# Operands of a blocked triangular inverse: two wide tiles filled by two engines, and the fourth pair's substitution on VectorE

## The chip, the cores and the metric

The kernel runs on one core of one Trainium2 chip. The metric is the device time of one execution in microseconds, the median of three runs. TensorE (PE) does matmuls, VectorE (DVE), ScalarE (ACT) and GpSimd (POOL) the elementwise work, SyncE (SP) issues the transfers.

## The reference

One layer of a hybrid backbone over 640 tokens (128 context, 512 latent), width 1024: one input projection, a bidirectional gated DeltaNet with 8 heads, a convolution branch, gates, an output projection and a SwiGLU block. What matters here is the DeltaNet: in each chunk a unit lower triangular system is solved.

```python
decay = jnp.exp(jnp.where(incl, gc[..., :, None] - gc[..., None, :], -jnp.inf))
a_mat = jnp.where(strict, jnp.einsum('bhnik,bhnjk->bhnij', kb, k) * decay, 0.0) \
    + jnp.eye(CHUNK, dtype=jnp.float32)
sol = lax.linalg.triangular_solve(a_mat, rhs, left_side=True, lower=True, unit_diagonal=True)
```

## The kernel before, in words

Heads are worked in four pairs. A pair has 20 matrices of 128x128 (2 directions d, 2 heads, 5 chunks) in the tile `Bt`, each to be inverted. `pair_prep` builds `Bt` (GpSimd sets its diagonal, line 590), takes the 32x32 diagonal blocks of all 20 into `Cc` (lines 598 and 599), transposes them into `M` (601) and inverts them by forward substitution: 30 steps of two elementwise instructions each (lines 610 and 612) on `X`, each step on the result of the one ahead. The table `SUBST_V` says which engine does them: VectorE for the first three pairs, GpSimd for the fourth. Two transposes (616, 617) leave the block inverses as `T1` and `T2`.

`pair_inverse` sets the 32x32 inverses into block diagonal 128x128 operands, `XA` and `XB`, in float16, one tile of four matrices for each of five lanes: a memset of `XA` on GpSimd (625) and the copies of line 631 on ScalarE. `XB` is zeroed once, at line 447. Each lane (`invert`) then takes six steps: GpSimd takes the part of `Bt` outside the diagonal blocks into `ct` (654); two products with `XA`, put into `a` and `atr` by ScalarE (665, 666); a product with `XB`, added to `XB` by VectorE (668), and a square put back into the lane's own `XA` (669); a third product (671); a transpose (675, 677) and the residual, by VectorE (678); the last product into `Bt` (680). All these matmuls but the last two steps' are of line 660. `pair_scan` uses the result (716 to 766), and `pair_out` follows.

In between runs the dense work, above all the projections: `load_w` fetches a weight tile `wr`, ScalarE rounds it to `wh` and VectorE or GpSimd takes the remainder `wl` (109, 110), and 48 matmuls of line 147 follow for each of some 50 column blocks. Their results leave through ScalarE and VectorE (873 and 875 for the gate `tz`, 882 for `tgt`); the convolution's 31 taps (847, 850 and 854) run on VectorE.

Generators (`preps`, `inverses`, `scans`, `mains` and others) are run turn about by the weights `W_...` that they yield; what a pair's chain issues has a higher priority than the dense work. A scheduler with a timeline of its own then fixes each engine's order of instructions when the kernel is built. On the chip every engine takes its list in that order and waits where an operand isn't ready.

## Time and profile before

| | before |
|---|---|
| median of 3 runs | 1381.05 us (1378.54 to 1384.46) |
| profiled execution, its own time | 1383.22 us |
| its span | 1381.2 us |
| PE, DVE, ACT, POOL busy | 94%, 61%, 39%, 22% |
| PE busy between 200 and 300 us | 80.97 us |
| PE busy between 900 us and the end | 470.99 of 481.20 us |

Busy shares are means over the span. The work that this case is about lies between 140 and 820 us; from 900 us on stand the feed-forward blocks. Since PE takes its list in order, what counts is where it stands idle, for whom it waits there, and at what clock it runs afterwards (the profile's column PEclk is the clock that was granted, 1.00 being full speed).

### The profile page before, as it was taken

To read this page: it belongs to the slowest core of one execution; us is meant where nothing else is said; L and a number is where in the kernel's file an instruction comes from. 1 tells how busy PE (TensorE), PEld (TensorE's weight loads), DVE (VectorE), ACT (ScalarE), POOL (GpSimd) and SP (SyncE) were. 2 spreads that over 40 slices of the span, in tenths; PEclk is the share of its full clock that TensorE was granted. 3 is DMA by queue.
4 is the path that set the end of the run, shared out by engine and by line. 5 is a ranking of instruction groups with operands and counts; after the bars stand their busy time and mean duration, and the time that the engine had idled before them with its cause. 6 is when DMAs were issued, how large, how long until landed. Compare 5 with 4: busy or idle time off the path is not lost.

```text
span 1381.2 us, 23408 instructions
## 1 busy us (share of the span) xinstructions
PE 1291.9 (94%) x9180; PEld 1213.3 (88%) x9180; DVE 839.1 (61%) x1603; ACT 542.0 (39%) x1240; POOL 306.8 (22%) x354
## 2 busy tenths in 40 slices
PE   4998996978999998988999989999999999999997
PEld 4998895977998998888989988889998999989996
DVE  5788985978667899596577774731223321233236
ACT  3337647263454555526454133332221222212223
POOL 2103310200010310291010025433310333003314
PEclk8999998999999999998999999999999999999999
DMA  9523442343343543323346884122222222222222
GB/s 289 140 64 113 125 149 80 112 136 100 113 119 99 160 118 94 103 66 94 118 150 212 250 284 148 46 74 77 77 77 76 77 77 77 76 76 69 71 77 91
DMA packets 180334, 157.31 MB, mean 114 GB/s; under 512 B 9072, under 2 KB 151809, under 8 KB 180225
## 3 DMA queue, kind: packets, MB, share of 16 engines
q1 hardware_dynamic: 180225, 155.83, 36.5%
q8 instruction: 72, 1.18, 0.4%
q14 instruction: 37, 0.30, 0.1%
HBM read 131.80 MB, written 24.00 MB: 113 GB/s over the span
## 4 chain that ended last, share of the span: by engine, by line
PE 68%; DVE 13%; ACT 6%; DMA 5%; issue 4%; POOL 1%; SPq 1%; POOLq 0%; DVEq 0%; ACTq 0%
PE mm L147 46%; PE sm L1115 9%; PE mm L1115 4%; DMA wr<-in_w_in 3%; ACT XA L631 2%; ACT XB L631 2%; PE sm L660 2%; DVE wl L110 1%; DVE uacc L847 1%; DVE acc L484 1%; PE sm L736 1%; ACT wh L109 1%; PE sm L495 1%; PE mm L469 1%; DMA og<-ogd 1%
## 5 line engine op out<-in xcount | busy, mean ns | idle before, releaser
L109 ACT ACTIVATE wh<-wr 128x1024 fp32r<-128x1024 f32 (+1 forms) x154 | 152.6, 992 | 497.5 <-PE mm L147 209.3
L147 PE MATMUL mm<-hh,wh 128*128 128x256 f32 (+1 forms) x896 | 219.7, 320 | 11.6 <-ACT wh L109 7.8
L147 PE MATMUL mm<-hl,wh 128*128 128x256 f32 (+1 forms) x896 | 218.0, 317 | 0.0
L147 PE MATMUL mm<-hh,wl 128*128 128x256 f32 (+1 forms) x896 | 216.4, 317 | 0.0
L110 POOL TENSOR_TENSOR wl<-wr,wh 128x1024 fp32r<-128x1024 f32 (+1 forms) x59 | 133.2, 2260 | 345.9 <-ACT wh L109 337.5
L110 DVE TENSOR_TENSOR wl<-wr,wh 128x1024 fp32r<-128x1024 f32 (+1 forms) x95 | 110.0, 1158 | 126.0 <-ACT wh L109 114.9
L147 PEld LDWEIGHTS mm<-hh,wh 128*128 128x128 f32 x896 | 163.5, 192 | 17.7 <-ACT wh L109 8.3
L147 PE MATMUL mm<-h2h,wh 128*128 128x256 f32 (+1 forms) x704 | 165.0, 312 | 1.5 <-ACT h2h L109 1.5
L147 PEld LDWEIGHTS mm<-hl,wh 128*128 128x128 f32 x896 | 166.3, 192 | 0.0
L147 PE MATMUL mm<-h2l,wh 128*128 128x256 f32 (+1 forms) x704 | 164.9, 312 | 0.9 <-POOL h2l L110 0.9
L147 PEld LDWEIGHTS mm<-hh,wl 128*128 128x128 f32 x896 | 164.6, 191 | 0.5 <-DVE wl L110 0.2
L147 PE MATMUL mm<-h2h,wl 128*128 128x256 f32 (+1 forms) x704 | 164.3, 311 | 0.3 <-DVE wl L110 0.3
L1253 DVE TENSOR_TENSOR ft<-ft,mm 128x384 f32<-128x384 f32 (+1 forms) x44 | 19.7, 484 | 198.8 <-PE mm L147 198.6
L147 PEld LDWEIGHTS mm<-h2l,wh 128*128 128x128 f32 x704 | 130.5, 191 | 1.1 <-POOL h2l L110 1.1
L147 PEld LDWEIGHTS mm<-h2h,wh 128*128 128x128 f32 x704 | 129.2, 190 | 1.9 <-ACT h2h L109 1.7
L147 PEld LDWEIGHTS mm<-h2h,wl 128*128 128x128 f32 x704 | 130.0, 190 | 0.6 <-DVE wl L110 0.6
L484 DVE SCALAR_TENSOR_TENSOR acc<-ci,colA,acc 128x642 f32<-128x642 f32 x96 | 85.9, 895 | 7.8 <-ACT acc L482 7.2
L1115 PE MATMUL sm<-wh,fl 128*128 128x512 f32 x152 | 60.0, 395 | 0.0
L1115 PE MATMUL sm<-wh,fh 128*128 128x512 f32 x152 | 59.9, 394 | 0.0
L1115 PE MATMUL sm<-wl,fh 128*128 128x512 f32 x152 | 59.7, 392 | 0.0
L110 DVE TENSOR_TENSOR fl<-ft,fh 128x640 fp32r<-128x640 f32 x22 | 47.7, 2167 | 15.5 <-ACT fh L109 15.5
L847 DVE SCALAR_TENSOR_TENSOR uacc<-u,colB,uacc 128x113 f32<-128x113 f32 (+14 forms) x120 | 47.8, 399 | 0.9
(341 smaller groups left out, 2431.7 us busy)
## 6 DMA issues: line engine op xcount, KB each, us to landing
wr<-in_w_in SPq DMA_DIRECT2D x56, 512.0 KB
wr<-in_w_gu SPq DMA_DIRECT2D x44, 512.0 KB
wr<-in_w_ada SPq DMA_DIRECT2D x32, 512.0 KB
wr<-in_w_down SPq DMA_DIRECT2D x22, 512.0 KB
wada<-in_w_ada SPq DMA_DIRECT2D x8, 1024.0 KB
atd<-et SPq DMA_DIRECT2D x40, 128.0 KB
aux<-atd SPq DMA_DIRECT2D x40, 128.0 KB
tgd<-tgt SPq DMA_DIRECT2D x16, 320.0 KB
```

The lines of the kernel that those rows point to most:

```text
L109: S_.activation(hi, x, AF.Identity)
L110: return (lo_eng or V).tensor_tensor(out=lo, in0=x, in1=hi.bitcast(F32), op=ALU.subtract)
L147: PE.matmul(out, a[:, kt, :], x, start=(kt == 0 and j == 0), stop=(kt == nk - 1 and j == 2))
L469: PE.matmul(pa[32 * g:32 * g + 32, :], sc[:, kt, o:o + 32], w[:, c:c + P], start=(bb == 0), stop=(bb == 1), tile_position=(0, 32 * g))
L484: V.scalar_tensor_tensor(out=acc[:, :n], in0=ci[:, k:k + n], scalar=vA[:, k, ct:ct + 1], in1=acc[:, :n], op0=ALU.mult, op1=ALU.add)
L495: PE.transpose(pt[:, c, :], src(c0 + c), ident)
L631: S_.activation(dst[r, o:o + cnt, 32 * b:32 * b + 32], src[r, :, n0:n0 + cnt].rearrange("p o n -> p n o"), AF.Identity)
L660: PE.matmul(pt[:, j, :], lhs[j], rhs[:, j, :], start=True, stop=True)
L736: PE.matmul(pv[:, d, j, :], Y1[:, d, j, ck[d], :], rhs, start=True, stop=True)
L847: V.scalar_tensor_tensor(out=acc[:, a0:128 - a1], in0=u[:, a0 + dl:128 - a1 + dl], scalar=tap(k, t4), in1=acc[:, a0:128 - a1], op0=ALU.mul ...
L1115: PE.matmul(acc[i], a[kt // 4][:, kt % 4, c], b[:, k2, :], start=(kt == 0 and j == 0), stop=(kt == nk - 1 and j == 2))
L1253: V.tensor_tensor(out=d, in0=d, in1=s, op=ALU.mult)
```

## The change

`XA` and `XB` become one tile each for all five lanes, indexed by direction and matrix, and each 32-row block is filled by one copy of 10 matrices: 8 copies for `XA` on ScalarE and 8 for `XB` on GpSimd, in place of 48 smaller ones on ScalarE. A lane takes its four matrices as a slice. The memset of `XA` becomes one instruction, that of `XB` too. The table `SUBST_V` goes, and all four substitutions are VectorE's.

```diff
-SUBST_V = (1, 1, 1, 0)
...
-    XA = [const(f"XA{i}", [P, 4, P], F16, s1p) for i in range(5)]
-    XB = [const(f"XB{i}", [P, 4, P], F16, s1p) for i in range(5)]
-    for t in XB:
-        G.memset(t, 0.0)
+    XA, XB = (const(nm, [P, 2, 10, P], F16, s1p) for nm in ("XA", "XB"))
+    G.memset(XB.rearrange("p d n i -> p (d n i)"), 0.0)
...
-            (V if SUBST_V[p] else G).tensor_tensor(out=t, in0=bc(M[:, j + 1:, j:j + 1], [P, n, j]), in1=bc(X[:, j:j + 1, 0:j], [P, n, j]),
+            V.tensor_tensor(out=t, in0=bc(M[:, j + 1:, j:j + 1], [P, n, j]), in1=bc(X[:, j:j + 1, 0:j], [P, n, j]),
                             op=ALU.mult)
-            (V if SUBST_V[p] else G).tensor_tensor(out=X[:, j + 1:, 0:j], in0=X[:, j + 1:, 0:j], in1=t, op=ALU.add)
+            V.tensor_tensor(out=X[:, j + 1:, 0:j], in0=X[:, j + 1:, 0:j], in1=t, op=ALU.add)
...
-        groups = [((0, 4, k % 2, 4 * (k // 2)),) for k in range(4)] + [((0, 2, 0, 8), (2, 2, 1, 8))]
-        for k, parts in enumerate(groups):
-            G.memset(XA[k], 0.0)
-            for o, cnt, d, n0 in parts:
-                n0 += 10 * d
-                for b in range(4):
-                    r = slice(32 * b, 32 * b + 32)
-                    for dst, src in ((XA[k], T1 if d == 0 else T2), (XB[k], T2 if d == 0 else T1)):
-                        S_.activation(dst[r, o:o + cnt, 32 * b:32 * b + 32],
-                                      src[r, :, n0:n0 + cnt].rearrange("p o n -> p n o"), AF.Identity)
-            yield W_BUILD
+        G.memset(XA.rearrange("p d n i -> p (d n i)"), 0.0)
+        for d in range(2):
+            for b in range(4):
+                r = slice(32 * b, 32 * b + 32)
+                S_.activation(XA[r, d, :, 32 * b:32 * b + 32],
+                              (T1, T2)[d][r, :, 10 * d:10 * d + 10].rearrange("p o n -> p n o"), AF.Identity)
+                G.tensor_copy(XB[r, d, :, 32 * b:32 * b + 32],
+                              (T2, T1)[d][r, :, 10 * d:10 * d + 10].rearrange("p o n -> p n o"))
+            yield 2.5 * W_BUILD
...
-            xa, xb = XA[k], XB[k]
...
+                xa, xb = XA[:, d, n0:n0 + 4, :], XB[:, d, n0:n0 + 4, :]
...
+                xa, xb = XA[:, :, 8:10, :], XB[:, :, 8:10, :]
```

The lists of the engines change with it. In the rows below a line of the changed kernel is 1 to 4 lower than the same line before (109 is 108, 738 is 734, 873 is 869, 665 is 661, 678 is 674, 847 is 843, 654 is 653, 612 is 609, and 631 is 624 on ScalarE and 626 on GpSimd).

ScalarE at the first pair's build. Before, the last of 48 copies and what stood behind them (`Cc` belongs to the second pair's preparation):

```order
L631 ACTIVATE XA_684<-T_1592 32x2x32
L631 ACTIVATE XB_689<-T_1591 32x2x32
L665 ACTIVATE L_672<-sm 128x512
L666 ACTIVATE L_673<-sm 128x512
L598 ACTIVATE Cc<-Bt 32x320 x4
L873 ACTIVATE tz<-mm 128x256
L873 ACTIVATE tz<-mm 128x384
```

Now, from the weights ahead of the copies to the first products:

```order
L108 ACTIVATE wh<-wr_59 128x1024
L624 ACTIVATE XA<-T_1579 32x10x32 x4
L869 ACTIVATE tz<-mm 128x256
L624 ACTIVATE XA<-T_1580 32x10x32 x4
L595 ACTIVATE Cc<-Bt 32x320 x4
L869 ACTIVATE tz<-mm 128x384
L108 ACTIVATE wh<-wr_55 128x1024
L661 ACTIVATE L_672<-sm 128x512
```

Eight copies stand where 48 stood, and the gate's first half is taken out between them.

ScalarE at the second pair's build, before (the first pair's scan has begun; `vn` is its):

```order
L631 ACTIVATE XA_684<-T_2552 32x2x32
L631 ACTIVATE XB_689<-T_2551 32x2x32
L109 ACTIVATE wh<-wr_59 128x1024
L738 ACTIVATE vn<-sm 128x512
L873 ACTIVATE tz<-mm 128x256
L873 ACTIVATE tz<-mm 128x384
```

and now:

```order
L108 ACTIVATE wh<-wr_59 128x1024
L734 ACTIVATE vn<-sm 128x512
L624 ACTIVATE XA<-T_2503 32x10x32 x4
L624 ACTIVATE XA<-T_2504 32x10x32 x4
L869 ACTIVATE tz<-mm 128x256
L869 ACTIVATE tz<-mm 128x384
```

The weights `wh` and the scan's `vn` have moved from behind the copies to ahead of them.

VectorE at the third pair's residuals (678, now 674), beside which the fourth pair's substitution runs. Before, the third and the fourth residual, among the convolution's taps (847):

```order
L678 TENSOR_TENSOR L_678<-sm,ident 128x512
L847 SCALAR_TENSOR_TENSOR uacc<-u,colB,uacc 128x116
L847 SCALAR_TENSOR_TENSOR uacc<-u,colB,uacc 128x115
L847 SCALAR_TENSOR_TENSOR uacc<-u,colB,uacc 128x114
L847 SCALAR_TENSOR_TENSOR uacc<-u,colB,uacc 128x113
L110 TENSOR_TENSOR wl_60<-wr_59,wh 128x1024
L678 TENSOR_TENSOR aux<-sm,ident 128x512
```

and now the same two:

```order
L674 TENSOR_TENSOR L_678<-sm,ident 128x512
L850 SCALAR_TENSOR_TENSOR uacc<-u,colB,uacc 128x448
L607 TENSOR_TENSOR stmp<-M,X 128x238
L843 SCALAR_TENSOR_TENSOR uacc<-u,colB,uacc 128x121
L850 SCALAR_TENSOR_TENSOR uacc<-u,colB,uacc 128x384
L609 TENSOR_TENSOR X<-X,stmp 128x17x14
L843 SCALAR_TENSOR_TENSOR uacc<-u,colB,uacc 128x122
L850 SCALAR_TENSOR_TENSOR uacc<-u,colB,uacc 128x320
L607 TENSOR_TENSOR stmp<-M,X 128x240
L843 SCALAR_TENSOR_TENSOR uacc<-u,colB,uacc 128x123
L674 TENSOR_TENSOR aux<-sm,ident 128x512
```

The substitution's steps (607, 609) now alternate with pairs of taps. Between the start of the fourth pair's substitution and the fourth residual stood 44 taps; now 21 taps and 29 steps of the substitution stand there.

## The prediction, as put on record before the changed kernel ran

> **What bounds the kernel now.** I read the page's busy shares first, then PE's own waits, then ScalarE's groups and timeline around the longest of them, and last a table of windows for the granted clock.

> ```profile
> PE 1291.9 (94%) x9180; PEld 1213.3 (88%) x9180; DVE 839.1 (61%) x1603; ACT 542.0 (39%) x1240; POOL 306.8 (22%) x354
> ```

> PE is the bound and has 1381.2 - 1291.9 = 89 us idle in its span. The change touches no matmul, so it can only give or take such idle time, and what the clock loses after it. The list of PE's waits (in all, times, longest) shows whom it waits for:

> ```profile
> PE mm L147 <- ACT wh L109: 8.9, 3, 7.1
> PE sm L566 <- ACT K L540: 6.5, 1, 6.5
> PE sm L660 <- ACT XA L631: 5.2, 2, 3.8
> ...
> PE mm L147 <- DVE tz L875: 3.8, 1, 3.8
> PE sm L660 <- DVE aux L678: 3.5, 1, 3.5
> PE sm L736 <- ACT Sn L749: 3.4, 1, 3.4
> ...
> PE sm L660 <- ACT L L665: 2.9, 1, 2.9
> PE sm L660 <- DVE L L678: 2.8, 2, 2.0
> ```

> Only one of these names the copies of line 631, but the others stand behind them. ScalarE's timeline at the second pair (start, us, engine, line), and PE's at the same place, show how:

> ```profile
> 275.78 0.44 ACT L631 ACTIVATE XA<-T 32x128 f16<-32x128 f32 x1 [5.21 <-DVE T L616]
> ...
> 291.31 0.29 ACT L631 ACTIVATE XB<-T 32x64 f16<-32x64 f32 x1
> 291.62 1.06 ACT L109 ACTIVATE wh<-wr 128x1024 fp32r<-128x1024 f32 x1
> ```
> ```profile
> 292.73 0.90 PE L147 MATMUL mm<-hh,wh 128*128 128x256 f32 x2 [7.08 <-ACT wh L109]
> ```

> For 15.84 us (275.78 to 291.62) ScalarE does nothing but copies, and the weights `wh` that PE needs stand behind the 48th. The third pair's 6.5 us (`K`, line 540) and the fourth's 3.4 us (`Sn`, line 749, which stands among the last copies) are of the same kind; the first pair's 5.2, 2.9 and 3.8 us are waits for the copies, for the first evacuation behind them, and for a gate that ScalarE took late. The windows behind the five places give the price that isn't in the list, the clock (columns: window, length, busy of each engine, PEclk, DMA):

> ```profile
> 221.00:237.00 16.00, 9.27 (x60) 8.15 (x60) 8.99 (x19) 13.23 (x31) 1.26 (x1) 0.57 0.23 75
> 290.00:298.00 8.00, 5.27 (x22) 5.04 (x23) 4.81 (x11) 4.07 (x12) 0.00 (x0) 0.57 0.70 233
> 552.00:560.00 8.00, 4.90 (x27) 4.28 (x26) 1.64 (x2) 7.91 (x25) 0.00 (x0) 0.57 0.22 84
> 620.00:628.00 8.00, 4.22 (x25) 4.09 (x25) 6.49 (x11) 0.00 (x0) 6.02 (x15) 0.57 0.21 82
> 648.00:656.00 8.00, 6.52 (x28) 6.53 (x29) 5.10 (x14) 6.49 (x21) 0.00 (x0) 0.57 0.36 117
> ```

> In each PE is granted 0.57 of its clock, so of its busy time 43% is lost: 4.0, 2.3, 2.1, 1.8 and 2.8 us.

> **The copies.** ScalarE's groups, shapes apart (count | busy, mean ns):

> ```profile
> L631 ACT ACTIVATE XA<-T 32x128 f16<-32x128 f32 x64 | 26.1, 425 | 9.7 <-DVE T L616 9.1
> L631 ACT ACTIVATE XB<-T 32x128 f16<-32x128 f32 x64 | 25.1, 413 | 0.1
> L631 ACT ACTIVATE XA<-T 32x64 f16<-32x64 f32 x32 | 9.7, 302 | 0.2
> L598 ACT ACTIVATE Cc<-Bt 32x320 f32<-32x320 f32 x16 | 7.5, 466 | 1.1 <-POOL Bt L590 1.0
> ```

> A copy of 32x320 with the strided read of line 631 isn't in the trace. From below it costs the 0.47 us of the same size in runs of 32 (line 598); from above 2.5 copies of 128, 1.06 us. The slope from 64 to 128 elements, (425 - 302)/64 = 1.9 ns, carried on from 425 gives 0.79 us, and I take that, for it is the same read. Eight are 6.3 us where 15.8 us stood: ScalarE is free 9.5 us sooner at each of four pairs.

> What becomes of the waits:
> - First pair: 5.2 + 2.9 + 3.8 = 11.9 us idle. `XA` of a direction is whole after four copies, 3.2 us; few matmuls stand between the lanes' first products, so up to 2 x 3.2 us of waiting can stay and none need; I keep 5. Gain 6.9, and the clock's 4.0, since none of the five windows lies behind waits as short as these would be.
> - Second pair: `wh` and `vn` now stand ahead of the copies. 7.1 + 2.3 = 9.4. Late next is the gate behind eight copies, but PE has a block of 48 matmuls in hand.
> - Third pair: `K` stands behind eight copies and one half gate instead of 48 copies. 6.5 + 2.1 = 8.6.
> - Fourth pair: `Sn` is now ahead of the copies. 3.4 + 2.8 = 6.2.

> [...]

> **The substitution.** On GpSimd it held the shared work of both engines back. Windows of the taps' two lines alone (DVE busy and count), while GpSimd ran the substitution and after it, and windows of the substitution's own tile `stmp` (DVE, then POOL):

> ```profile
> 580.00:627.00 47.00, 17.29 (x30) 0.94 0.24 74
> 638.00:662.00 24.00, 4.43 (x13) 0.86 0.40 119
> ```
> ```profile
> 580.00:627.00 47.00, 12.64 (x14) 0.94 0.24 74
> 638.00:662.00 24.00, 6.12 (x12) 0.86 0.40 119
> ```
> ```profile
> 468.00:535.00 67.00, 19.92 (x60) 0.00 (x0) 1.00 0.44 127
> 579.00:628.00 49.00, 0.00 (x0) 35.00 (x60) 0.93 0.23 71
> ```
> ```profile
> 577.00:633.00 56.00, 48.40 (x381) 46.43 (x380) 48.48 (x73) 15.99 (x28) 45.50 (x72) 0.94 0.22 66
> ```

> Taps of line 847 take 17.29/30 = 0.58 us beside GpSimd and 4.43/13 = 0.34 alone; those of 854 0.90 and 0.51. So the 44 taps get 7.1 + 5.5 = 12.6 us shorter, and the 60 steps cost VectorE 19.9 us (the third pair's row; 35.0 on GpSimd). Net +7.3 us on a VectorE that is busy 48.5 of 56 us: it fills up and just fits, so the transposes 616 and 617 come about when they did. What moves is the residual. Ahead of its fourth stand 11 and 10 taps and 29 steps, 11 x 0.34 + 10 x 0.51 + 29 x 0.33 = 18.4 us, where 29.9 us of taps stood: 11 us sooner, and PE waited 3.5 + 2.0 us there. Gain 5.5 + 1.8 = 7.3 us. Were the taps not to get shorter, the fourth pair would be 12.6 us later.

> **GpSimd's copies.** A GpSimd copy isn't in the trace. Rows that bound it:

> ```profile
> L654 POOL TENSOR_TENSOR L<-Bt,off 128x512 f16<-128x512 f32 x12 | 16.1, 1357 | 0.2 <-DVE L L671 0.2
> L604 POOL TENSOR_SCALAR_AFFINE_SELECT X<-M 128x1024 f32<-128x1024 f32 x4 | 6.9, 1734 | 32.3 <-DVE M L601 32.3
> L612 POOL TENSOR_TENSOR X<-X,stmp 128x234 f32<-128x234 f32 x2 | 2.5, 1250 | 0.1
> ```

> Per element 1.7, 2.7 and 5.3 ns, so 320 elements take 0.54 to 1.7 us; I take line 654's 0.85, which also writes float16. Eight are 6.8 us (4.3 to 13.7). `XB` is first read late:

> ```profile
> 208.04 1.21 DVE L617 STREAM_TRANSPOSE T<-X 128x1024 f32<-128x1024 f32 x1
> ```
> ```profile
> 236.34 0.40 PE L660 MATMUL sm<-XB,L 128*128 128x128 f16 x4
> ```

> 27.1 us after the transpose's end, 17.6 when ScalarE's 9.5 are off. The copies are hidden behind that, and the cover is gone at 2.2 us each. [...] While they run, VectorE's taps are slower by 0.58/0.34: up to 0.7 x 6.8 = 4.7 us a pair, 19 in all, none if PE waits for no tap; PE rarely does, so I take 4. The memsets are the same bytes.

> **What a faster PE runs into.** ScalarE already waits for weights:

> ```profile
> ACT wh L109 <- DMA wr<-in_w_in: 40.9, 19, 11.9
> ```

> A PE that is 40 us ahead asks for these sooner. Between nothing and all of 40.9 I take 5, because PE itself waits for `wh` three times only.

> **The sum.** 10.9 + 9.4 + 8.6 + 6.2 + 7.3 = 42.4, less 4 and 5, is 33 us. The profiled execution took 1383.2 us (span 1381.2, 2.0 around it), 2.2 above the median; 1383.2 - 33 = 1350.

> **The rivals.**
> - *The weights take over.* PE catches up with the loads, and what the first two places give is waited for again at the next `wh`. Against it: PE has only 8.9 us of waits for `wh`, 7.1 of them behind the copies. About half is left, 16 us: 1367.
> - *VectorE becomes the bound at the fourth pair.* Taps stay long or the steps wait for each other, the transposes come 12.6 us late, and PE idles for the fourth scan; the residual's 7.3 are not gained either. 33 - 20 = 13 us: 1370. For it: VectorE at 48.5 of 56 us; against: the taps' two rows.
> - *No change.* PE reaches the same later waits, on the scans, at the same time. Against it: between 650 and 800 us PE stands idle little. 1381.
> - *Slower: GpSimd's copies are late.* PE waits for `XB` in its list, 8p - 17.6 us at each of four pairs. At p = 2.2 us it begins, and 33 + 7 us are eaten at p = 3.5 us; at 4 us it is 58 - 33 = 25 us slower, 1406. Against it: the slowest row gives 1.7 us.

> **How the numbers follow.** Forecast 0.60, the weights 0.14, VectorE 0.10, no change 0.07, GpSimd 0.07, and 0.02 for what I don't see. Half a per cent, 6.9 us, is about what a measurement of this kernel can tell from no change. Faster by more are the first three, 0.82 with a little taken off for small sizes; within it 0.09, slower 0.09. The range goes from the full 42.4 us with 3 us of spread between runs (1336) to the VectorE case with as much again beside it (1376).

> **What would show it.** Right: 32x320 copies at 0.8 us on ScalarE and under 1.2 on GpSimd; no wait of PE over 3 us for `wh`, `K` or `Sn`; the five windows at a clock near 1; taps near 0.34 us beside the fourth substitution, save while `XB` is copied. Wrong: PE waits for `XB`, or for line 678's place, or for the fourth pair's `T`, or new waits for `wh` on transfers.

## The result and the profile after

The changed kernel takes 1344.16 us (median of 4 runs, 1341.94 to 1345.64), the kernel before beside it 1382.35 us. The ratio is 0.9725, with a 95% interval of 0.9705 to 0.9745: 38 us, or 2.7%, faster. A second comparison on another chip (below, the changed kernel again) gave 0.9698 (0.9676 to 0.9719). The forecast was 1350 us.

The page's busy times and PE's list of waits (in all, times, longest), after:

```profile
PE 1279.7 (95%) x9180; PEld 1204.2 (90%) x9180; DVE 845.6 (63%) x1663; ACT 505.2 (38%) x1080; POOL 299.9 (22%) x306
```
```profile
PE sm L742 <- DVE vw L738: 4.2, 2, 2.5
PE sm L659 <- ACT XA L624: 3.5, 2, 2.2
...
PE mm L146 <- ACT sh L108: 3.0, 1, 3.0
...
PE mm L146 <- ACT wh L108: 1.1, 2, 0.7
...
PE sm L712 <- ACT Sn L745: 1.0, 1, 1.0
...
PE sm L659 <- DVE aux L674: 0.7, 1, 0.7
```

The span is 1344.0 us where it was 1381.2. PE is idle for 64.3 us of it, 25.0 less than before, and the same 9180 matmuls take 1279.7 us, 12.2 less: 37.2 us, two thirds from waits and one third from PE's busy time. Of those 12.2 us the clock makes 9.5, an estimate that counts half of PE's busy time in the stretches that were granted 0.50 (pairs of 128x256 matmuls of line 146 start 0.53 us apart in the one at 217 us and 0.29 apart right behind it, at 220.4 us): these are 41.7 us long in all, where they were 74.0. `wh` has gone from 8.9 to 1.1, the wait for `K` of 6.5 is no longer in the list, `Sn` and line 678's `aux` (now 674) are under 1.1. Between 140 and 820 us the first in the list is now `vw`, a wait for VectorE, and it was not forecast (longer ones stand ahead of 110 us, at the start of the program).

The new copies, the taps beside the fourth pair's substitution (lines 847 and 854, now 843 and 850), the substitution's tile, and all engines over the same time (count, or busy and count of PE, PEld, DVE, ACT, POOL):

```profile
L624 ACT ACTIVATE XA<-T 32x320 f16<-32x320 f32 x32 | 25.0, 781 | 10.7 <-DVE T L613 10.4
...
L626 POOL CAST XB<-T 32x320 f16<-32x320 f32 x32 | 26.5, 827 | 26.7 <-DVE T L613 25.4
```
```profile
555.00:612.00 57.00, 9.80 (x30) 1.00 0.33 94
```
```profile
555.00:612.00 57.00, 6.56 (x14) 1.00 0.33 94
```
```profile
557.00:612.00 55.00, 21.57 (x60) 1.00 0.34 96
```
```profile
555.00:612.00 57.00, 56.35 (x452) 55.47 (x450) 56.31 (x147) 18.38 (x35) 10.92 (x8) 1.00 0.33 94
```

The copies were priced at 0.79 and 0.85 us and take 0.78 and 0.83. Taps of line 843 take 9.80/30 = 0.33 us (0.58 before), those of line 850 6.56/14 = 0.47 (0.90 before). The substitution's 60 instructions take 21.6 us, and VectorE is busy 56.31 of 57 us while PE is busy 56.35: it fills up, and PE waits 0.7 us for it (`aux`).

ScalarE's timeline at the second pair, where `wh` stood behind 48 copies, and the windows that answer to the five of the prediction (window, length, busy of each engine, PEclk, DMA); the third of the six is a new place within the second pair:

```profile
270.24 1.06 ACT L108 ACTIVATE wh<-wr 128x1024 fp32r<-128x1024 f32 x1 [9.17 <-DMA wr<-in_w_in]
272.20 0.60 ACT L734 ACTIVATE vn<-sm 128x512 f32<-128x512 f32 x1 [0.91 <-PE sm L732]
274.82 6.36 ACT L624 ACTIVATE XA<-T 32x320 f16<-32x320 f32 x8 [2.02 <-DVE T L613]
```
```profile
216.00:224.00 8.00, 8.00 (x65) 7.31 (x63) 4.29 (x5) 7.37 (x15) 0.07 (x1) 0.79 0.30 95
...
288.00:296.00 8.00, 8.00 (x75) 7.60 (x75) 8.00 (x23) 2.52 (x5) 0.00 (x0) 1.00 0.36 120
...
304.00:312.00 8.00, 5.74 (x46) 5.16 (x47) 7.18 (x21) 3.55 (x8) 0.00 (x0) 0.79 0.36 126
```
```profile
536.00:544.00 8.00, 7.96 (x63) 7.54 (x62) 8.00 (x19) 3.16 (x11) 0.00 (x0) 1.00 0.29 94
...
584.00:592.00 8.00, 7.35 (x60) 7.16 (x59) 8.00 (x21) 1.71 (x3) 0.00 (x0) 1.00 0.37 111
...
616.00:624.00 8.00, 7.56 (x55) 7.30 (x54) 4.87 (x13) 6.71 (x11) 4.66 (x6) 1.00 0.65 201
```

The clock is at 1.00 at four of the five old places, and 0.79 in one window at the first pair. New places stand at 304 us, in the scan beside the second pair, and at 322 us a little later (0.79 in the windows from there); a sixth place of before, at 727 us, has gone, and 0.79 is met again at 712 and at 776 us, behind waits for `sh` (3.0 us) and `oh` (2.67, shown further on).

**Where along the program the time was gained.** To set two kernels side by side I take the starts of the weights tiles `wh` on ScalarE in the order in which they come: the 25th, for example, starts at 345.46 us before and at 333.15 us after, so the changed kernel is 12.3 us ahead there. The table gives for each kernel the change of this difference to the kernel before, in us, from one such tile to the next named; negative is gained. The 17th tile starts at 204 us, the 81st at 837 us of the kernel before. Every row is one profiled execution.

```
                        first pair  second   third   residuals   tail
tile                       17-21     21-25   25-50   + 4th 50-74  74-81
forecast                   -10.9      -9.4    -8.6      -13.5       -
changed                    -10.4      -2.7    -5.3      -20.6     +1.9
changed, again             -10.5      -3.7    -6.5      -21.2     +1.7
copies alone               -10.8      -4.2    -4.6      -14.7    +12.5
substitution alone          -1.4      +0.8    -2.8       -3.3     +1.5
XB on ScalarE               -5.4      -1.7    -1.7      -11.7     +2.0
XB twice                   -14.1     +13.0    -0.9      -11.0     -0.4
no taps, second pair       -10.8      -7.8    -6.4      -18.6     +1.7
no taps, third pair        -10.1      -2.7    -7.1      -19.9     +2.0
blocks 3 gates later        -9.5      -2.7    -2.1      -23.9     +8.9
XB on VectorE              -10.0      -8.0    -7.7      -18.2     +1.9
XB on VectorE, again        -8.9      -6.3    -7.6      -15.5     +3.0
  and 1 gate later          -9.7      -6.8    -6.5      -18.6    +11.1
wide at the fourth only     +0.1      +0.2    -1.7      -13.0    +11.6
```

The 9 us that the forecast takes off its sum stand in no column. Two executions of one program agree within about 1.7 us in a column up to the 50th tile, and within 2.7 in the fourth.

A start on ScalarE need not be the same place in PE's list. PE's own row between the marks of the first four columns, before and then after (window, length, PE busy and its matmuls, PEclk, DMA):

```profile
203.56:256.97 53.41, 41.47 (x348) 0.87 0.32 99
256.97:345.46 88.49, 75.84 (x671) 0.96 0.35 111
345.46:601.80 256.34, 245.91 (x1966) 0.99 0.38 112
601.80:808.65 206.85, 190.43 (x1429) 0.96 0.52 164
```
```profile
204.36:247.33 42.97, 39.46 (x348) 0.96 0.39 122
247.33:333.15 85.82, 77.19 (x672) 0.96 0.37 115
333.15:584.23 251.08, 247.30 (x2002) 1.00 0.39 114
584.23:770.45 186.22, 178.97 (x1390) 0.99 0.57 181
```

By the 50th tile the changed kernel has done 36 matmuls more, of the last steps of the third pair's inverse, and 39 fewer follow up to the 74th. So the column 25-50 shows too small a gain and 50-74 too large a one. What does not hang on that is what the prediction added up: the time that PE stands idle (length less busy) and what the clock costs it (half of its busy time in the stretches granted 0.50). Their change to the kernel before, both together:

```
                        first pair  second   third   residuals   tail
tile                       17-21     21-25   25-50   + 4th 50-74  74-81
forecast                   -10.9      -9.4    -8.6      -13.5       -
changed                    -10.3      -2.8    -8.9      -14.0     +1.7
changed, again             -10.0      -4.2    -9.9      -15.5     +1.4
copies alone               -10.4      -4.3    -8.3       -6.3    +11.3
substitution alone          -1.2      +0.9    -2.3       -2.3     +0.4
XB on ScalarE               -2.9      -2.7    -3.9       -8.9     +0.8
no taps, second pair       -10.1      -7.7    -9.8      -12.5     +1.5
no taps, third pair         -9.2      -2.8   -10.1      -15.4     +0.8
XB on VectorE               -9.5      -6.8    -9.6      -16.0     +2.0
XB on VectorE, again        -8.8      -5.1    -9.6      -13.0     +2.0
```

For the changed kernel the columns add up to 34.3 us, of 37.1 between the 17th and the 81st tile; the rest is PE's busy time at full clock, and is not explained.

### The profile page after: what moved, and what is told of

Its sections match the earlier page's. It is cut to its first block, busy times and chain, and to the rows that moved or that the text cites. A ratio compares the mean times of both kernels' runs of the same rounds, so it can differ in the third digit from the quotient of the medians.

```text
span 1344.0 us, 23244 instructions
## 1 busy us (share of the span) xinstructions
PE 1279.7 (95%) x9180; PEld 1204.2 (90%) x9180; DVE 845.6 (63%) x1663; ACT 505.2 (38%) x1080; POOL 299.9 (22%) x306
## 4 chain that ended last, share of the span: by engine, by line
PE 58%; DVE 8%; issue 2%; DMA 2%; ACT 2%; POOL 1%; POOLq 0%; SPq 0%; DVEq 0%; ACTq 0%
PE mm L146 37%; PE sm L1111 9%; PE mm L1111 4%; DVE wl L109 1%; PE sm L732 1%; DVE uacc L846 1%; PE sm L659 1%; PE sm L756 1%; PE sm L712 1%; DVE uacc L843 1%; PE sm L719 1%; PE sm L742 1%; PE sm L1156 1%; POOL x L1207 1%; PE mm L466 1%
## 5 line engine op out<-in xcount | busy, mean ns | idle before, releaser
L146 PE MATMUL mm<-hh,wl 128*128 128x256 f32 (+1 forms) x896 | 212.6, 314 | 0.0
L109 POOL TENSOR_TENSOR wl<-wr,wh 128x1024 fp32r<-128x1024 f32 (+1 forms) x59 | 133.1, 2257 | 354.3 <-ACT wh L108 327.2
L109 DVE TENSOR_TENSOR wl<-wr,wh 128x1024 fp32r<-128x1024 f32 (+1 forms) x95 | 110.6, 1164 | 112.0 <-ACT wh L108 100.8
L109 DVE TENSOR_TENSOR fl<-ft,fh 128x640 fp32r<-128x640 f32 x22 | 47.6, 2165 | 15.3 <-ACT fh L108 15.3
L607 DVE TENSOR_TENSOR stmp<-M,X 128x30 f32<-128x30 f32 (+14 forms) x120 | 44.4, 370 | 2.5 <-POOL X L601 1.0
```

The costliest lines, as they stand in the source:

```text
L109: return (lo_eng or V).tensor_tensor(out=lo, in0=x, in1=hi.bitcast(F32), op=ALU.subtract)
L146: PE.matmul(out, a[:, kt, :], x, start=(kt == 0 and j == 0), stop=(kt == nk - 1 and j == 2))
L607: V.tensor_tensor(out=t, in0=bc(M[:, j + 1:, j:j + 1], [P, n, j]), in1=bc(X[:, j:j + 1, 0:j], [P, n, j]), op=ALU.mult)
```

## The experiments

### Copies and substitution apart

```diff
-            V.tensor_tensor(out=t, ...
+            (V if p < 3 else G).tensor_tensor(out=t, ...
...
-            V.tensor_tensor(out=X[:, j + 1:, 0:j], ...
+            (V if p < 3 else G).tensor_tensor(out=X[:, j + 1:, 0:j], ...
```

> The changed kernel with the fourth pair's substitution back on GpSimd, so that only the wide copies are new. If the parts add up as in the prediction (copies 35.1 us less the deductions, substitution 7.3): 1344 + 7 = 1351 us, and PE waits again 2.0 and 3.5 us for the third pair's residuals. If the substitution counts for nothing once the copies are short: 1344. If GpSimd's substitution holds the taps back enough to make VectorE late for the fourth pair as well: 1356 or more.

Measured: 1361.43 us, ratio 0.9845 (0.9826 to 0.9865): 21 us faster than before, 17 slower than the changed kernel.

In the kernel before:

```diff
-SUBST_V = (1, 1, 1, 0)
+SUBST_V = (1, 1, 1, 1)
```

> The kernel before with the fourth pair's substitution on VectorE and nothing else. If the parts add up: 1381 - 7.3 = 1374 us, the waits for the third pair's residuals gone and those for K (6.5) and wh (7.1) still there. If what it gives is eaten at the fourth pair's copies, which still hold ScalarE for 15.8 us: 1381. If VectorE gets too full: slower than 1381.

Measured: 1377.18 us, ratio 0.9954 (0.9936 to 0.9972): 6 us faster, near the 7.3 forecast.

21 and 6 make 27, not 38. PE's timeline with the copies alone, its waits at the third pair's residuals and, 190 us later, where the fourth pair's output meets the output projection:

```profile
585.44 0.44 PE L659 MATMUL sm<-L,L 128*128 128x128 f16 x5 [1.64 <-DVE L L674]
592.08 0.91 PE L659 MATMUL sm<-L,L 128*128 128x128 f16 x7 [6.20 <-DVE aux L674]
```
```profile
777.92 1.06 PE L146 MATMUL mm<-oh,wh 128*128 128x256 f32 x2 [3.19 <-DVE ta L908]
781.66 2.39 PE L791 MATMUL sm<-ident,oacc 128*128 128x128 f32 x10 [2.68 <-DVE oacc L779]
785.41 0.90 PE L146 MATMUL mm<-ol,wh 128*128 128x256 f32 x2 [1.15 <-DVE ol L109]
789.15 1.12 PE L146 MATMUL mm<-oh,wh 128*128 128x256 f32 x3 [1.24 <-ACT oh L108]
```

The first two are the waits that the substitution takes away. They are 1.64 and 6.20 us where 2.0 and 3.5 were expected. The second group is new: 8.3 us of waits, with the clock at half behind them (0.59 and 0.50 in the windows from 776 and 784 us). In the changed kernel these transposes (line 791) stand 12 us ahead of the last product that waits, with other columns' matmuls between, and only 2.67 us are waited for:

```profile
762.92 1.25 PE L791 MATMUL sm<-ident,oacc 128*128 128x128 f32 x10
775.34 0.57 PE L146 MATMUL mm<-oh,wh 128*128 128x256 f32 x2 [2.67 <-ACT oh L108]
```

The first table shows that this tail makes up the surplus: from the 17th to the 74th tile copies alone gain 34.3 us on the kernel before and the substitution alone 6.7, together 41.0, and the whole change 39.0. The parts nearly add up there (by the second table 34.2 us, and 36.0 or 39.6 in the changed kernel's two executions); the copies alone then lose 12.5 us in the tail. By the second table the substitution is worth more beside the wide copies than alone (14.0 or 15.5 less 6.3, against 2.3), for with the narrow ones a wait for `wh` takes its place.

### XB's copies on ScalarE too

```diff
-                G.tensor_copy(XB[r, d, :, 32 * b:32 * b + 32],
-                              (T2, T1)[d][r, :, 10 * d:10 * d + 10].rearrange("p o n -> p n o"))
+                S_.activation(XB[r, d, :, 32 * b:32 * b + 32],
+                              (T2, T1)[d][r, :, 10 * d:10 * d + 10].rearrange("p o n -> p n o"), AF.Identity)
```

> The changed kernel with the eight copies of XB on ScalarE too: 16 wide copies at 0.78 us, 12.5 us a pair in place of 6.3 (and of 15.8 before); what stands around them on ScalarE keeps its place in the list. If it is ScalarE's time that counts, 3.3 of 9.5 us are left at each pair and about two thirds of the copies' gain of some 30 us goes: 1364. If what counts is that wh, vn and Sn now stand ahead of the copies, only the first pair pays, some 6 us: 1350.

Measured: 1361.83 us, ratio 0.9847 (0.9828 to 0.9867), 17 us slower than the changed kernel. PE's waits:

```profile
PE mm L146 <- ACT wh L108: 7.3, 5, 3.3
...
PE sm L659 <- ACT XA L624: 6.6, 2, 4.4
...
PE sm L563 <- ACT L L661: 3.7, 1, 3.7
```

It is ScalarE's time that counts: the second half of the 32x320 copies costs 17 us. By the second table 7 us of it are lost at the first pair and 5 each at the third and the fourth, where the instructions around the copies keep their place in the list, or nearly so. At the second pair they don't: `vn` stands behind the copies again, and a `wh` among them. Nothing more is lost there, so that place tells nothing of the two cases.

### GpSimd's copies twice

```diff
                 G.tensor_copy(XB[r, d, :, 32 * b:32 * b + 32],
                               (T2, T1)[d][r, :, 10 * d:10 * d + 10].rearrange("p o n -> p n o"))
+                G.tensor_copy(XB[r, d, :, 32 * b:32 * b + 32],
+                              (T2, T1)[d][r, :, 10 * d:10 * d + 10].rearrange("p o n -> p n o"))
```

> The changed kernel with each of GpSimd's copies done twice, 13.2 us a pair in place of 6.6. XB is first read 10.8, 29.6, 19.9 and 21.0 us after the last copy, so it comes in time in all pairs and only VectorE's instructions beside the copies pay. By the prediction's 4 us for that: 1348. If that cost is smaller, as the two slowed taps of the second pair say (0.9 us): 1345. If XB's cover is shorter than the trace makes it look: over 1355.

Measured: 1364.0 us, ratio 0.9863 (0.9845 to 0.9881), over 1355 as the third case has it, but not for its reason. Nowhere does PE wait over 0.4 us for `XB`. The loss is 13 us at the second pair, where PE waits for `XA`; PE's and VectorE's timelines:

```profile
305.89 0.58 PE L661 MATMUL sm<-XA,L 128*128 128x128 f16 x4 [9.97 <-ACT XA L624]
```
```profile
299.83 0.19 DVE L609 TENSOR_TENSOR X<-X,stmp 128x30 f32<-128x30 f32 x1
...
300.79 1.90 DVE L613 STREAM_TRANSPOSE T<-X 128x1024 f32<-128x1024 f32 x1
...
305.43 0.81 DVE L845 SCALAR_TENSOR_TENSOR uacc<-u,colB,uacc 128x119 f32<-128x119 f32 x1
306.16 1.20 DVE L848 SCALAR_TENSOR_TENSOR uacc<-u,colB,uacc 128x440 f32<-128x440 f32 x1
...
315.26 1.11 DVE L717 SCALAR_TENSOR_TENSOR r<-sm,neg_eg,K 128x128 f32<-128x128 f32 x4
```

With eight more instructions a pair the build set VectorE's list otherwise: the taps stand among the second pair's substitution, and `T` comes at 300.8 us instead of 272.7. So this run does not price what was meant. It shows two other things: when `T` is late, the second pair waits for it, and taps beside GpSimd's copies take 0.81 and 1.20 us where they take 0.33 and 0.67 elsewhere.

### Taps left out beside the second pair, and beside the third

```diff
+            if t4 != 0:
-            V.scalar_tensor_tensor(out=acc[:, a0:128 - a1], in0=u[:, a0 + dl:128 - a1 + dl], scalar=tap(k, t4),
-                                   in1=acc[:, a0:128 - a1], op0=ALU.mult, op1=ALU.add)
+                V.scalar_tensor_tensor(out=acc[:, a0:128 - a1], in0=u[:, a0 + dl:128 - a1 + dl], scalar=tap(k, t4),
+                                       in1=acc[:, a0:128 - a1], op0=ALU.mult, op1=ALU.add)
```

> The changed kernel without the 30 taps of line 843 in the first block of the convolution, which stand between the second pair's scan steps on VectorE (30 x 0.34 = 10.2 us of its work). That part of the convolution is left out, the order of what is left stays. If VectorE's list sets the second pair's scan once the copies are short, most of the 7 us that the second pair gave back come: 1337 to 1339. If the scan's own chain from engine to engine sets it: 1344.

The other has `if t4 != 1:` there.

> The changed kernel without the 30 taps of line 843 in the second block of the convolution, beside the third pair's preparation and inverse. The same 10.2 us are left out where PE was busy 69.5 of 70 us. If VectorE binds only where PE waits for it: 1343 to 1344. If 10 us of VectorE's work are worth the same anywhere: as much as leaving them out beside the second pair.

Measured: 1340.38 us, ratio 0.9694 (0.9649 to 0.9740), and 1349.0 us, 0.9746 (0.9716 to 0.9777). By the totals neither can be told from the changed kernel. By the place they can, with one execution each: at the second pair the kernel without its taps gains 7.8 us, the four executions that have them in the same places 2.7, 3.7, 4.2 and 2.7 (changed twice, copies alone, no taps at the third pair). Idle time and clock say the same: 7.7 against 2.8, 4.2, 4.3 and 2.8. PE's waits at the two scan steps, changed kernel first:

```profile
305.94 1.22 PE L742 MATMUL sm<-vw,K 128*128 128x128 f32 x4 [2.48 <-DVE vw L738]
...
319.48 0.71 PE L742 MATMUL sm<-vw,K 128*128 128x128 f32 x4 [1.68 <-DVE vw L738]
```
```profile
303.80 0.71 PE L742 MATMUL sm<-vw,K 128*128 128x128 f32 x4 [1.47 <-DVE vw L738]
...
314.42 0.71 PE L742 MATMUL sm<-vw,K 128*128 128x128 f32 x4 [1.21 <-DVE vw L738]
```

The same 10.2 us left out beside the third pair change its column by 0.6 to 1.8 us (0.2 to 1.2 in the second table), little more than two executions of one program differ by. So VectorE's list binds at the second pair, 3.5 to 5 us of it, and not at the third.

### The convolution's blocks later

```diff
-GLU_AT = (7, 11, 16, 19)
+GLU_AT = (10, 13, 17, 20)
```

> The changed kernel with GLU_AT = (10, 13, 17, 20) for (7, 11, 16, 19): the convolution's blocks start three, two, one and one gates later. Between the second pair's second and fourth scan step stand 13 taps where 49 stood, the rest goes behind them. All work is done. If VectorE's list is what the second pair waits for, its 7 us come: 1337. If the taps are missed later, where the third and fourth pair now have them beside their scans: 1350 or more.

Measured: 1351.8 us, ratio 0.9765 (0.9730 to 0.9799). The second pair gains nothing by it (2.7 as before). PE's waits there are now 1.52 us for `S` and 1.70 for `vw`: the inverse's own steps come beside the scan's, and I take it that they wait for the taps in their turn, which no run tests. Up to the 74th tile it is even with the changed kernel; the tail loses 8.9.

### XB's copies on VectorE

```diff
-                G.tensor_copy(XB[r, d, :, 32 * b:32 * b + 32],
+                V.tensor_copy(XB[r, d, :, 32 * b:32 * b + 32],
```

> The changed kernel with the eight copies of XB on VectorE in place of GpSimd. If GpSimd's copies cost by slowing the taps beside them (4 us in the prediction) and eight copies on VectorE are short (0.4 us): 1342 to 1344. If VectorE's time in the second pair is what counts, 3 us or more for the copies come on top: 1347 or more.

Measured: 1341.37 us, ratio 0.9698 (0.9669 to 0.9728). The copy's row:

```profile
L626 DVE CAST XB<-T 32x320 f16<-32x320 f32 x32 | 14.1, 442 | 0.3
```

To see whether this is a better version, three kernels were measured side by side on one chip; the third of them has `GLU_AT = (8, 11, 16, 19)` beside the copies on VectorE.

> The changed kernel as it is, on one chip with the next two, so that their few microseconds can be compared: 0.9725 of the kernel before.

> XB's copies on VectorE, as in the run before, with more rounds. If the 5.9 us that its trace was ahead from the second pair on are real: 0.968 of the kernel before, 6 us under the changed kernel. If they were spread between runs: 0.972.

> As the one above, with GLU_AT = (8, 11, 16, 19) for (7, 11, 16, 19): the first block's taps start one gate later and run on past the second pair's scan, the rest of the list is the same. If VectorE still holds the second pair: 1 to 2 us less than the one above. If nothing is left there: the same.

Measured: 1343.04 us, 0.9698 (0.9676 to 0.9719); 1344.01 us, 0.9702 (0.9679 to 0.9724); 1353.12 us, 0.9781 (0.9758 to 0.9805). Copies on VectorE are the same as on GpSimd: what they gain at the second pair (6.3 to 8.0 against 2.7 to 3.7) is not in the total. One gate later loses 11.1 us in the tail. No version was found that beats the changed kernel.

### The wide copies at the fourth pair alone

```diff
-    def pair_inverse(R):
+    def pair_inverse(R, p):
...
+        if p == 3:
+            (the changed kernel's 16 copies)
+        else:
+            (48 copies on ScalarE, in the order of the kernel before, into the wide tiles)
```

> The substitution on VectorE and the wide copies at the fourth pair alone; the first three pairs have 48 narrow copies on ScalarE as before. Substitution alone gave 6 us, copies alone 21, both 38: 11 us more than the sum. If that surplus is made at the fourth pair, where the substitution alone only turned the residuals' wait into a wait for wh behind 48 copies (6.9 us and the clock after it): 6 + 11 us and the 6.2 of the place itself, 1360. If the fourth pair's place is worth just what the prediction gave it: 6 + 6.2, 1371. If the surplus needs the first three pairs' earlier start: 1376.

Measured: 1379.19 us, ratio 0.9982 (0.9966 to 0.9998): above all three. By the first table the middle one was near up to the 74th tile, 12.2 us forecast (6 and 6.2) against 14.4. Then the tail takes 11.6 back. PE's waits there are 2.92 us (for `ta`), 2.93 (`oacc`), 1.40 (`ol`) and 1.14 (`oh`): the four of the copies alone, at the same place in the program.

So what I took for a surplus of the two parts together is a matter of how the list ends: in four of the eleven changed kernels, those with 8.9 us or more in the last column of the first table, PE waits 6.4 to 8.4 us where the fourth pair's output is due, and with the clock behind that it costs 9 to 12.5 us. That PE has little else left to do there is my reading of the lists. Which edit brings it about I can't say: it comes and goes with edits far from it, and no run changed the tail alone.

## Why the prediction was right, point by point

- **Bound and mechanism.** Right. PE's idle time and the clock behind it were what could be gained: 25.0 us less idle and 12.2 less busy came, where the prediction's terms for its five places hold 29.4 and 13.0. The terms below are held against the second table, in the prediction's own measure.
- **First pair.** Forecast 10.9, measured 10.3 and 10.0. `XA` is waited for 3.5 us, not the 5 kept. The 4.0 us of clock did not all come: a window at 0.79 (1.7 us lost) stands behind waits of 1.27 and 2.24 us. That none of the five windows lies behind waits so short is true of the five. But the trace of before has a sixth place, at 727 us, where the clock falls behind a wait of 1.87 us (last section), and the prediction left it out.
- **Second pair.** This is the term that was mis-sized: 9.4 forecast, 2.8 and 4.2 measured. The wait for `wh` went as forecast. But VectorE had stood idle for the same `wh`, as its timeline of before shows:

```profile
292.71 1.23 DVE L110 TENSOR_TENSOR wl<-wr,wh 128x1024 fp32r<-128x1024 f32 x1 [6.62 <-ACT wh L109]
```

  It too has no stall to lose now, is busy 8.00 of 8 us from 288 us on, has taps in its list between the scan's steps, and PE waits for `r` and `vw` (1.2, 2.48 and 1.68 us, where it waited twice 1.2 for `vw` before), with two stretches at half clock behind them (3.41 us each, from 306 and 326 us), and one in the second execution. The prediction looked for what is late next only at the gate behind the copies. Left-out taps gave 3.5 to 5 us of it back; the rest is not explained.
- **Third pair.** 8.6 forecast, 8.9 and 9.9 measured. `K`'s wait is gone and the clock is at 1.00. The smaller 5.3 and 6.5 of the first table hold the 36 matmuls that now stand ahead of its mark.
- **Residuals and fourth pair.** 13.5 forecast together, 14.0 and 15.5 measured. It is not quite the same sum, though. From 590 us on (574 after), to the end of the third pair's output, PE was idle 15.4 us and 3.6 after, so waits further on in that output, which the prediction did not count (1.9 us for `oacc`, and 1.7 for the clock behind it), went too. Against them stands a new wait, 3.0 us for `sh` at 715 us and the clock behind it, where before 1.0 us was waited, for `wh`, at the same place. Substitution alone gave 2.3 here, for it turned the residuals' wait into one for `wh` behind 48 copies, 6.90 us:

```profile
659.06 0.91 PE L147 MATMUL mm<-hh,wh 128*128 128x256 f32 x2 [6.90 <-ACT wh L109]
```

- **GpSimd's copies, 4 us taken off.** In the total no such loss was found. VectorE's part of it is real (at the third pair six taps and a `wl` beside the copies are 3.7 us longer), but PE waits for none of it there, and the kernel with copies on VectorE, which has none of it, takes the same time. At the second pair that kernel is 1 to 4 us further ahead; whether GpSimd's copies are the reason there, no run shows.
- **The weights, 5 us taken off.** PE's wait for `wh` fell to 1.1 us in all; the weights' transfers did not become the bound.
- **The sum.** 33 us forecast, 38 measured. The first pair, the third, and the residuals with the fourth gave 33.2 and 35.4 us where 33.0 were forecast. The second pair is 5 to 7 us short, and the 9 taken off were not found as such; the tail loses under 2. So one term was too large, and a deduction of about the same size stood for losses that did not come: that the total lies so near is in that part luck.

## What to carry to other kernels

When one engine's stall is taken away, ask of every engine that stalled with it what stands in its list behind that point: here VectorE had been waiting for the same weights, and about half of what was to be gained at that place became waits for VectorE. Merging small copies pays by the engine's time, not by their number alone: 48 into 16 on one engine gave 21 us with the substitution, 48 into 8 and 8 on two engines 38. And where a scheduler fixes the lists, an edit can move things far from itself (here 9 to 12.5 us at the end of the last pair), so compare two kernels place by place, not by their totals alone. A mark on one engine can move against another's list (here by 36 matmuls): compare the idle time and the clock of the engine that bounds the kernel, not only the time between marks.

## What the runs showed of the hardware that was not expected

A tap on VectorE (it reads `u` and `uacc`) takes 0.81 us beside a GpSimd copy and 0.33 alone, a longer one 1.20 and 0.67; `r`, whose first operand is the matmuls' `sm`, takes 1.11 us for four beside the copies and 1.11 elsewhere. The two taps lost 0.5 us each beside the copies, over half of a copy's 0.83; no run shows why.

```profile
723.48:726.89 3.41, 1.24 (x7) 1.00 0.50 146
726.89:730.31 3.42, 3.42 (x22) 0.51 0.33 123
```
```profile
302.19:305.61 3.42, 1.26 (x16) 1.00 0.48 152
305.61:309.02 3.41, 3.08 (x16) 0.50 0.25 97
```
```profile
299.87:303.28 3.41, 1.97 (x26) 1.00 0.40 121
303.28:306.69 3.41, 2.34 (x24) 1.00 0.33 129
```

In the first slice of the first two blocks PE is idle 2.2 us, and the next slice is granted 0.51 and 0.50. In the last block it is idle 1.4 and 1.1 us, and the clock stays at 1.00. Between 130 and 900 us of the fourteen traces no stretch at half clock has less than 1.48 us of idle time in the slice ahead, and no slice with more than 1.90 us is followed by full clock; in between both occur. Before the change a slice with 3.41 - 1.67 = 1.74 us of idle time, from 214.94 us, is followed by 1.00; after it one with 3.41 - 1.74 = 1.67 us, from 322.70 us, is followed by 0.50:

```profile
214.94:218.35 3.41, 1.67 (x18) 1.00 0.31 81
218.35:221.76 3.41, 1.17 (x14) 1.00 0.24 73
```
```profile
322.70:326.11 3.41, 1.74 (x19) 1.00 0.91 266
326.11:329.52 3.41, 3.41 (x18) 0.50 0.59 165
```

So PE was not idle through the whole slice ahead of a stretch at half clock: 1.67 of 3.41 us were enough there.

The strided 32x320 copy takes 0.78 us on ScalarE, 0.83 on GpSimd and 0.44 on VectorE; the same size in runs of 32 takes 0.47 on ScalarE.
